# Building one-hot pairs for eight tokens at a time, with new schedule constants

## The chip, the cores and the metric

The kernel runs on one core of one Trainium2 chip. The metric is the device time of one execution in microseconds (us), taken as the median of several runs. TensorE does the matrix products, VectorE and ScalarE the elementwise work, GpSimd issues the gathering transfers, and the queues of SyncE and ScalarE issue the other transfers.

## The reference

A two-layer decoder trunk over 512 tokens plus 16 meta tokens, width 1024, all in float32. Layer 0 mixes with causal pooling, layer 1 with stick-breaking attention over a shared K and V. Behind each stands a PEER feed-forward, which is what the change touches:

```python
def peer(h, w_query, sub_keys, u, v):        # per chunk of tokens
    q = einsum('btd,dq->btq', hx, w_query)   # 8 heads, 2 halves of 128
    s = einsum('bthpc,hpnc->bthpn', q, sub_keys)
    top_s, top_i = top_k(s, 16)              # per half, of 128 sub-keys
    cand = top_s[..., 0, :, None] + top_s[..., 1, None, :]
    best_s, best_pos = top_k(cand, 16)       # of 256 candidates
    expert = i1 * 128 + i2                   # the two sub-key indices of each
    gate = softmax(best_s)
    act = gelu(hx . u[expert])
    return sum(gate * act * v[expert])
```

There are 128 x 128 = 16384 experts a layer, and each token uses 8 heads x 16 = 128 of them.

## The kernel before

**Two ways to the experts.** Of the four tiles of 128 tokens, three are *dense*: every one of the 16384 experts is computed for all 384 tokens and weighted by a gate matrix that is zero nearly everywhere. The fourth tile (`GATHERED`), and in layer 0 the meta tokens, fetch their own experts' rows: one indirect transfer of 128 x 2048 floats (u and v side by side) brings one expert for each of 128 tokens, and VectorE does `prod` (line 355, the dot product), `gwt` (363) and `hx` (367, the weighted sum). These *row steps* are spread over the whole layer.

**Stages of a layer.** (1) The query projection: scores of the sub-keys and their top 16 for each head. (2) The gate stage, lines 600 to 640: for each of the three dense tiles `select` finds the 16 pairs of each head and looks up the two indices i1 and i2, and `build_gates` writes the gate matrix. (3) The value stage: 128 steps `v`, each of 18 matmuls of 512 columns into six accumulators.

**A u step** (`u_parts`, line 314) computes gelu(u . h) for 128 experts and 384 tokens with 24 matmuls: the weights are split into a high and a low part, `w_hi` by ScalarE (line 279) and `w_lo` by VectorE (line 281) once `gating` is set. A layer has 128 u steps. Those that run ahead of the value stage write their result to DRAM (`aout<-ac`) and the value stage loads it again; the rest run within the value stage.

**The gate matrix.** For each token there are 128 chosen pairs (i1, i2) with a gate. With the tokens' pairs on the partitions, the matrix [i2, i1] of one token is the product of the one-hots of i2 with the one-hots of i1 times the gate. The gate is split into two f16 parts, so each token takes two matmuls of 128x128 into a tile `pg`; ScalarE copies four tokens of pg at a time into `stage`, which goes to DRAM as `gout` each 32 tokens.

Before, VectorE builds this for `TG` = 4 tokens in four operations: line 596 the one-hot of i2 into ab[0], line 597 that of i1 into e1, lines 598 and 599 e1 times the two gate parts into ab[1] and ab[2]. `place` issues the matmuls `GLAG` = 2 groups later. ab has three buffers, e1 two.

**The index look-up** (lines 439 to 445) compares the position with 0..15 into a tile `oh` of 2048 elements, multiplies it by the indices and sums; oh has a buffer of its own.

**The order of work** in the gate stage is written out by a plan. `gate_stream` yields a cost in us for each piece of VectorE work. td adds it, times `DVE_SLACK`; tu adds 0.5 for each placed group and ucost/4 for each quarter of a u step; quarters are issued while tu is behind td. Row steps are issued while their own clock tr is behind td, each adding 18/8 to tr and 4.7/8 to td, and four of them make a row; they stop when fewer than `QUIET` groups are left. With `pinned` set, TensorE keeps this order. `issue_after` holds a row's VectorE operations behind the latest marked VectorE operation (`vmark`). Fewer u steps in the gate stage mean as many more in the value stage. In the projection, `ucost` also decides how many u steps fill in.

Of the kernel before, what the change touches and what calls it, by code (L numbers as in the profile page):

```python
# [20 lines left out]
P = 128  # L21
# [5 lines left out]
H = 8  # L27
NK = 128
TK = 16
# [5 lines left out]
GSCALE = 32768.0  # L35
NCAND = 80
TB = 32
FRONT = 3
UPARTS = 4
TG = 4  # L40
GLAG = 2
DVE_SLACK = 1.08
KLAG = 3
ALAG = 3
JG = 4
# [5 lines left out]
WQ_PE = (15.5, 12.5)  # L51
GATHERED = (3,)
LEAD = (2, 2)
QUIET = 16


@with_exitstack
def trunk_kernel(ctx: ExitStack, tc: tile.TileContext, x, meta, norm_mix, norm_ffn, pool_w, pool_scale,
                 kv_norm, w_kv, k_norm, w_q, q_norm, w_o, peer_wq, peer_keys, peer_ut, peer_uv, out):
    nc = tc.nc  # L60
    v, sc, pe, gp, sy = nc.vector, nc.scalar, nc.tensor, nc.gpsimd, nc.sync
# [4 lines left out]
    def const(shape, dt, name):  # L66
        return cp.tile(shape, dt, name=name)
# [1 line left out]
    ident = const([P, P], F32, "ident")  # L69
    make_identity(nc, ident)  # L70
    iota_x = const([P, P, 2], F16, "iota_x")
    iota_b = const([P, TK], BF, "iota_b")
    own = const([P, AH], F32, "own")
    rr = const([P, H, NM], F32, "rr")
    gkv = const([P, KC], F32, "gkv")
# [179 lines left out]
    def peer(layer, with_meta, gain, hn_nat, kp, up, finish):  # L255
# [5 lines left out]
        ND = nd * P  # L261
# [6 lines left out]
        with ExitStack() as cl:  # L268
# [3 lines left out]
            vmark, amark, pmark, todo = [], [], [], []  # L272
# [17 lines left out]
            def pin(x):  # L290
                return tc.keep_in_program_order(x) if pinned[0] else x
# [80 lines left out]
            def row_step():  # L372
                if not stepping:
                    if not todo:
                        return False
                    stepping.append(row_steps())
                if next(stepping[0], 0):
                    return True
                stepping.clear()
                return row_step()  # L380

            with ExitStack() as c1:
                tp = c1.enter_context(tc.tile_pool(name="tp", bufs=1, reuse_waits="tile"))
                ps1 = c1.enter_context(tc.tile_pool(name="ps1", bufs=2, reuse_waits="tile", space=PSUM))
# [14 lines left out]
                def select(tmp, outp, tag, tvi, tii, nh, res):  # L399

                    ns = nh * TK

                    def st(name, dt=F32):
                        return tmp.tile([P, H * TK], dt, name=name)[:, :ns]
# [12 lines left out]
                    a, b, u, w = st("da"), st("db"), st("du"), st("dw")  # L417
# [14 lines left out]
                    v.scalar_tensor_tensor(u, a, 16.0, u, ALU.mult, ALU.min)  # L432
                    vmark.append(v.tensor_sub(b, bp, u))
                    yield 3.5
                    tib = tmp.tile([P, nh, 2, TK], BF, name=f"tib{nh}")
                    v.tensor_copy(tib, tii)
                    for half, sel in ((0, a), (1, b)):
                        oh = tmp.tile([P, ns, TK], BF, name=f"oh{nh}")
                        v.tensor_tensor(oh, iota_b.unsqueeze(1).to_broadcast([P, ns, TK]),
                                        sel.unsqueeze(2).to_broadcast([P, ns, TK]), ALU.is_equal)  # L440
                        o4 = oh.rearrange("p (h s) a -> p h s a", h=nh)
                        v.tensor_tensor(o4, o4, tib[:, :, half, :].unsqueeze(2).to_broadcast([P, nh, TK, TK]),
                                        ALU.mult)
                        ir = outp.tile([P, ns], F32, name=f"{tag}i{half}")
                        v.tensor_reduce(ir, oh, AX.X, ALU.add)
                        res.append(ir)
                        yield 6.0 * nh / H
# [11 lines left out]
                    res.append(gate)  # L459
                    yield 1.0  # L460

                ucost = 0.0098 * ND + 0.15
                tq = tr = td = tu = 0.0
                j0 = 0
                with ExitStack() as cq:
# [28 lines left out]
                    for h in range(H):  # L494
                        qts = []
                        for pp in range(2):
                            hp = 2 * h + pp
                            w, whi, wlo = weight(plan.pop(), plan[-1])
# [51 lines left out]

                gb = c1.enter_context(tc.tile_pool(name="gb", bufs=1, reuse_waits="tile"))

                def build_gates(n, i1, i2, gate):

                    pt = ps1.tile([P, 4, P], F32, name="ps1")
                    for q, t in enumerate((i1, i2, gate)):
                        pe.transpose(pt[:, q, :], t, ident)
                    sl = gb.tile([P, 4, P], F16, name="sl", bufs=2)
                    sc.activation(sl[:, :2], pt[:, :2], AF.Copy)
                    sc.activation(sl[:, 2], pt[:, 2], AF.Copy, scale=GSCALE)  # L560
                    gf = gb.tile([P, P], F32, name="gf")
                    v.tensor_copy(gf, sl[:, 2])
                    v.scalar_tensor_tensor(sl[:, 3], pt[:, 2], GSCALE, gf, ALU.mult, ALU.subtract)
                    stages = {}

                    def place(t0, ab):
                        tb = t0 // TB
                        if tb not in stages:
                            stages[tb] = gb.tile([P, NK, TB], F32, name="stage", bufs=2)
                        stage = stages[tb]  # L570
                        pg = ps1.tile([P, TG, NK], F32, name="pg")
                        with tc.issue_after(pmark[-1].ins):
                            for q in range(TG):
                                a, b = divmod(q, 2)
                                pin(pe.matmul(pg[:, q, :], ab[:, 0, a, :, b], ab[:, 1, a, :, b],
                                                 start=True, stop=False))
                                pin(pe.matmul(pg[:, q, :], ab[:, 0, a, :, b], ab[:, 2, a, :, b],  # L577
                                                 start=False, stop=True))
                        pcost[0] += 0.5
                        o = t0 % TB  # L580
                        with tc.issue_after(amark[-1].ins):
                            sc.activation(stage[:, :, o:o + TG].rearrange("p j t -> p t j"), pg, AF.Copy,  # L582
                                                  scale=1.0 / GSCALE)
                        if o + TG == TB:
                            sc.dma_start(gout[:, n * (P // TB) + tb], stage)

                    waiting = []
                    for t0 in range(0, P, TG):
                        ab = gb.tile([P, 3, TG // 2, NK, 2], F16, name="ab", bufs=GLAG + 1)
                        e1 = gb.tile([P, TG // 2, NK, 2], F16, name="e1", bufs=2)  # L590
                        ix = iota_x.unsqueeze(1).to_broadcast([P, TG // 2, NK, 2])

                        def col(q):
                            pair = sl[:, q, t0:t0 + TG].rearrange("p (a b) -> p a b", b=2)
                            return pair.unsqueeze(2).to_broadcast([P, TG // 2, NK, 2])
                        v.tensor_tensor(ab[:, 0], ix, col(1), ALU.is_equal)  # L596
                        v.tensor_tensor(e1, ix, col(0), ALU.is_equal)  # L597
                        v.tensor_tensor(ab[:, 1], e1, col(2), ALU.mult)  # L598
                        vmark.append(v.tensor_tensor(ab[:, 2], e1, col(3), ALU.mult))  # L599
                        waiting.append((t0, ab))  # L600
                        if len(waiting) > GLAG:
                            place(*waiting.pop(0))
                        yield 1.34
                    for wq in waiting:
                        place(*wq)

# [2 lines left out]
                def gate_stream():  # L609
                    if with_meta:  # L610
                        res = []
                        yield from select(gb, gr, "gm", tvm, tim, 1, res)
                        gather_rows(NT, 0, *res, TK, ym, True)
                    for n, i in enumerate(dense):
                        res = []
                        yield from select(gb, gb, "gd", tv[i], ti[i], H, res)
                        for cost in build_gates(n, *res):
                            blocks[0] -= 1
                            yield cost

                pcost = [0.0]
# [434 lines left out]
```

## Time and profile before

| | |
|---|---|
| median of 3 runs | 3105.51 us (3097.78 to 3110.7) |
| the profiled execution: time, span | 3103.72 us, 3102.0 us |
| busy TensorE, its weight loads | 2942.2 us (95%), 2605.9 us (84%) |
| busy VectorE | 2446.9 us (79%) |
| busy ScalarE, GpSimd | 1349.8 us (44%), 734.9 us (24%) |
| mean granted clock of TensorE | 0.979 |

The span is the time from the first to the last instruction of the profiled execution. Busy shares are averages over stages with different limits; the records of neighbouring operations of one engine overlap a little, so a duration isn't always what an operation costs in a row of them. A "releaser" is what an engine's idle time ended with.

### The profile page before, as it was taken

Reading aid. Unit: us, or ns where it says so; the run is one execution under the profiler, and the core shown is the slowest. Engines: PE = TensorE matmul, PEld = TensorE weight load, DVE = VectorE, ACT = ScalarE, POOL = GpSimd, SP = SyncE. Lnnn points to the kernel's source line nnn. Section 1 sums busy time; section 2 is a strip of 40 time slices with the busy share of each in tenths; the row PEclk is TensorE's granted clock in tenths of the full one; section 3 lists DMA queues with packets and bytes.
Section 4 is the critical chain, followed back from the end, with each engine's and each line's share of the span. In section 5 each row is a group of like instructions: output and inputs, shape, how many; then the busy total and the mean of one; then the engine's idle time right before and its main releaser. Section 6 shows DMA issues by size and latency. Waiting matters only on the chain.

```text
span 3102.0 us, 45813 instructions
## 1 busy us (share of the span) xinstructions
PE 2942.2 (95%) x16514; PEld 2605.9 (84%) x16514; DVE 2446.9 (79%) x5636; ACT 1349.8 (44%) x2184; POOL 734.9 (24%) x704
## 2 busy tenths in 40 slices
PE   8988988999999999999999989798899999999999
PEld 7887888888888888879965778788888888888887
DVE  3999998987777778786456469999988777777765
ACT  3343655633333333344456334355655333333333
POOL 3431521311111111114245244322321111111100
PEclk9999999999999999999999999999999999999999
DMA  3535877899898998862100344477879998989875
GB/s 128 183 123 202 301 272 274 307 377 326 312 335 300 343 317 324 285 219 73 55 1 1 109 171 145 155 266 278 296 270 346 356 324 311 338 301 335 308 251 162
DMA packets 286709, 758.52 MB, mean 245 GB/s; under 512 B 23185, under 2 KB 176785, under 8 KB 248337
## 3 DMA queue, kind: packets, MB, share of 16 engines
q1 hardware_dynamic: 222544, 390.92, 37.5%
q0 software_dynamic: 39168, 285.23, 25.0%
q10 hardware_dynamic: 24768, 79.44, 6.5%
q8 instruction: 129, 2.11, 0.3%
q14 instruction: 100, 0.81, 0.1%
HBM read 673.99 MB, written 81.53 MB: 244 GB/s over the span
## 4 chain that ended last, share of the span: by engine, by line
PE 68%; DVE 26%; DMA 2%; issue 2%; ACT 2%; POOL 0%; SPq 0%; DVEq 0%; ACTq 0%; POOLq 0%
PE y L693 33%; PE psu L314 21%; DVE w_lo L281 3%; PE pp L124 2%; PE pp L125 2%; PE pp L123 2%; DVE prod L355 2%; DVE ab L599 2%; DVE ab L598 2%; DVE e L597 2%; DVE hx L367 2%; DVE ab L596 2%; DVE mr L395 1%; DVE ti L397 1%; DVE ti L394 1%
## 5 line engine op out<-in xcount | busy, mean ns | idle before, releaser
L343 POOL DMA_INDIRECT row<-in_peer_uv_dram,ei x272 | 429.0, 1577 | 1751.3 <-DVE hx L367 1406.2
L314 PE MATMUL psu<-n_hi,w_lo 128*128 128x384 f32 x2048 | 705.9, 345 | 64.4 <-DVE w_lo L281 62.4
L314 PE MATMUL psu<-n_hi,w_hi 128*128 128x384 f32 x2048 | 722.2, 353 | 11.5 <-ACT ac L321 7.2
L314 PE MATMUL psu<-n_lo,w_hi 128*128 128x384 f32 x2048 | 706.0, 345 | 0.6 <-DVE n_lo L118 0.6
L279 ACT ACTIVATE w_hi<-w 128x1024 fp32r<-128x1024 f32 x288 | 305.0, 1060 | 480.2 <-PE psu L314 378.3
L693 PE MATMUL y<-v_hi,wt_hi 128*128 128x512 f32 x1536 | 474.0, 390 | 1.2 <-ACT wt_hi L685 0.8
L693 PE MATMUL y<-v_hi,wt_lo 128*128 128x512 f32 x1536 | 473.9, 390 | 0.2
L693 PE MATMUL y<-v_lo,wt_hi 128*128 128x512 f32 x1536 | 473.5, 389 | 0.5 <-DVE v_lo L679 0.5
L314 PEld LDWEIGHTS psu<-n_hi,w_lo 128*128 128x128 f32 x2048 | 396.5, 194 | 73.5 <-DVE w_lo L281 71.1
L314 PEld LDWEIGHTS psu<-n_hi,w_hi 128*128 128x128 f32 x2048 | 394.9, 193 | 17.5 <-ACT ac L321 7.5
L314 PEld LDWEIGHTS psu<-n_lo,w_hi 128*128 128x128 f32 x2048 | 395.3, 193 | 5.5 <-DVE n_lo L118 1.1
L685 ACT ACTIVATE wt_hi<-wt 128x384 fp32r<-128x384 f32 x256 | 134.3, 525 | 576.4 <-PE y L693 294.9
L686 DVE TENSOR_TENSOR wt_lo<-wt,wt_hi 128x384 fp32r<-128x384 f32 x256 | 142.5, 557 | 263.8 <-ACT wt_hi L685 263.8
L693 PEld LDWEIGHTS y<-v_lo,wt_hi 128*128 128x128 f32 x1536 | 288.2, 188 | 61.8 <-DVE v_lo L679 1.3
L693 PEld LDWEIGHTS y<-v_hi,wt_lo 128*128 128x128 f32 x1536 | 288.1, 188 | 61.3 <-DVE wt_lo L686 1.1
L367 DVE SCALAR_TENSOR_TENSOR hx<-row,gwt,hx 128x1024 f32<-128x1024 f32 x256 | 334.5, 1307 | 2.1
L355 DVE SCALAR_TENSOR_TENSOR prod<-row,hnat 128x1024 bf16<-128x1024 f32 x272 | 335.7, 1234 | 0.4 <-DMA row<-in_peer_uv_dram,ei 0.4
L281 DVE TENSOR_TENSOR w_lo<-w,w_hi 128x1024 fp32r<-128x1024 f32 x228 | 278.1, 1220 | 72.8 <-ACT w_hi L279 71.3
L693 PEld LDWEIGHTS y<-v_hi,wt_hi 128*128 128x128 f32 x1536 | 286.6, 188 | 54.1 <-ACT wt_hi L685 1.4
L679 DVE TENSOR_TENSOR v_lo<-v,v_hi 128x1024 fp32r<-128x1024 f32 x256 | 312.2, 1220 | 6.9 <-ACT v_hi L678 6.8
L678 ACT ACTIVATE v_hi<-v 128x1024 fp32r<-128x1024 f32 x256 | 270.8, 1058 | 16.5 <-DMA v<-in_peer_uv_dram 13.6
L582 ACT ACTIVATE stage<-pg 128x512 f32<-128x512 f32 x192 | 211.7, 1133 | 103.5 <-PE pg L577 102.4
(313 smaller groups left out, 4518.0 us busy)
## 6 DMA issues: line engine op xcount, KB each, us to landing
w<-in_peer_ut_dram SPq DMA_DIRECT2D x256, 512.0 KB
v<-in_peer_uv_dram SPq DMA_DIRECT2D x256, 512.0 KB
gout<-stage ACTq DMA_DIRECT2D x24, 2048.0 KB
gt<-gout SPq DMA_DIRECT2D x64, 768.0 KB
aout<-ac ACTq DMA_DIRECT2D x148, 192.0 KB
ac<-aout SPq DMA_DIRECT2D x148, 192.0 KB
w<-in_peer_wq_dram SPq DMA_DIRECT2D x32, 512.0 KB
wn<-in_w_kv_dram SPq DMA_DIRECT2D x8, 1024.0 KB
```

Source lines behind the costliest of these rows:

```text
L279: amark.append(sc.activation(whi, w, AF.Copy))
L281: vmark.append(v.tensor_sub(wlo, w, whi.bitcast(F32)))
L314: m = pin(pe.matmul(ps[:, :ND], a[:, k, :], b[:, k, c0:c0 + ND], start=st, stop=en))
L343: gp.indirect_dma_start(out=row, out_offset=None, in_=peer_uv, in_offset=bass.IndirectOffsetOnAxis(ap=item[1], axis=0))
L355: v.scalar_tensor_tensor(prod, row[:, :D], 1.0, hn_nat[i], ALU.mult, ALU.mult, accum_out=dot)
L367: v.scalar_tensor_tensor(acc, row[:, D:], wt, acc, ALU.mult, ALU.add)
L582: sc.activation(stage[:, :, o:o + TG].rearrange("p j t -> p t j"), pg, AF.Copy, scale=1.0 / GSCALE)
L678: amark.append(sc.activation(vhi, v32, AF.Copy))
L679: vmark.append(v.tensor_sub(vlo, v32, vhi.bitcast(F32)))
L685: sc.activation(whi, wt, AF.Copy)
L686: vmark.append(v.tensor_sub(wlo, wt, whi.bitcast(F32)))
L693: pe.matmul(y[n][half], wp[:, ts], vq[:, half * 512:(half + 1) * 512], start=st, stop=en)
```

## The change

One-hots are made for eight tokens in three operations: one comparison writes the one-hots of i1 and i2 into a tile `hot`, and two multiplications write i1's one-hots times the two gate parts into `weighed`. For that the transposed columns `sl` are laid out by groups of eight tokens. hot and weighed have GLAG + 1 = 2 buffers each. The index look-up of the dense tiles takes a buffer of hot as its oh, and the look-up's small constants become f16. `place` now issues two pg tiles of four tokens. Constants of the plan change too: TG, GLAG, DVE_SLACK, QUIET, ucost, and the costs of a group and of a placement.

```diff
-TG = 4
-GLAG = 2
-DVE_SLACK = 1.08
+TG = 8
+GLAG = 1
+DVE_SLACK = 1.35
-QUIET = 16
+QUIET = 8
-    iota_b = const([P, TK], BF, "iota_b")
+    iota_b = const([P, TK], F16, "iota_b")
-                    tib = tmp.tile([P, nh, 2, TK], BF, name=f"tib{nh}")
+                    tib = tmp.tile([P, nh, 2, TK], F16, name=f"tib{nh}")
-                        oh = tmp.tile([P, ns, TK], BF, name=f"oh{nh}")
+                        if nh == H:
+                            oh = hot_tile().rearrange("p w a k b -> p (w a k b)").rearrange("p (n a) -> p n a", a=TK)
+                        else:
+                            oh = tmp.tile([P, ns, TK], F16, name=f"oh{nh}")
-                ucost = 0.0098 * ND + 0.15
+                ucost = 0.0111 * ND
+                def hot_tile():
+                    return gb.tile([P, 2, TG // 2, NK, 2], F16, name="hot", bufs=GLAG + 1)
-                    sl = gb.tile([P, 4, P], F16, name="sl", bufs=2)
-                    sc.activation(sl[:, :2], pt[:, :2], AF.Copy)
-                    sc.activation(sl[:, 2], pt[:, 2], AF.Copy, scale=GSCALE)
-                    gf = gb.tile([P, P], F32, name="gf")
+                    sl = gb.tile([P, P // TG, 2, 2, TG], F16, name="sl", bufs=2)
+                    for q in range(2):
+                        sc.activation(sl[:, :, 0, q, :], grouped(pt[:, q, :]), AF.Copy)
+                    sc.activation(sl[:, :, 1, 0, :], grouped(pt[:, 2, :]), AF.Copy, scale=GSCALE)
+                    gf = gb.tile([P, P], F32, name="dw")
...
-                        pg = ps1.tile([P, TG, NK], F32, name="pg")
-                            for q in range(TG):
-                        pcost[0] += 0.5
+                        for t in range(t0, t0 + TG, 4):
+                            pg = ps1.tile([P, 4, NK], F32, name="pg")
+                                for q in range(4):
+                            pcost[0] += 0.47
...
-                        ab = gb.tile([P, 3, TG // 2, NK, 2], F16, name="ab", bufs=GLAG + 1)
-                        e1 = gb.tile([P, TG // 2, NK, 2], F16, name="e1", bufs=2)
-                        ix = iota_x.unsqueeze(1).to_broadcast([P, TG // 2, NK, 2])
-                        v.tensor_tensor(ab[:, 0], ix, col(1), ALU.is_equal)
-                        v.tensor_tensor(e1, ix, col(0), ALU.is_equal)
-                        v.tensor_tensor(ab[:, 1], e1, col(2), ALU.mult)
-                        vmark.append(v.tensor_tensor(ab[:, 2], e1, col(3), ALU.mult))
-                        waiting.append((t0, ab))
+                        hot = hot_tile()
+                        weighed = gb.tile([P, 2, TG // 2, NK, 2], F16, name="weighed", bufs=GLAG + 1)
+                        c = sl[:, t0 // TG].rearrange("p q w (a b) -> p q (w a) b", b=2)
+                        v.tensor_tensor(hot.rearrange("p w a k b -> p (w a) k b"),
+                                        iota_x.unsqueeze(1).to_broadcast([P, TG, NK, 2]),
+                                        c[:, 0].unsqueeze(2).to_broadcast([P, TG, NK, 2]), ALU.is_equal)
+                        for part in range(2):
+                            m = v.tensor_tensor(weighed[:, part], hot[:, 0],
+                                                c[:, 1, part * TG // 2:(part + 1) * TG // 2].unsqueeze(2).to_broadcast(
+                                                    [P, TG // 2, NK, 2]), ALU.mult)
+                        vmark.append(m)
+                        waiting.append((t0, hot, weighed))
-                        yield 1.34
+                        yield 2.44
```

## Rows read from the trace of the kernel before

**Rows 1.** The page, part 4: the chain that ended last, by engine and line.
```profile
PE 68%; DVE 26%; DMA 2%; issue 2%; ACT 2%; POOL 0%; SPq 0%; DVEq 0%; ACTq 0%; POOLq 0%
PE y L693 33%; PE psu L314 21%; DVE w_lo L281 3%; PE pp L124 2%; PE pp L125 2%; PE pp L123 2%; DVE prod L355 2%; DVE ab L599 2%; DVE ab L598 2%; DVE e L597 2%; DVE hx L367 2%; DVE ab L596 2%; DVE mr L395 1%; DVE ti L397 1%; DVE ti L394 1%
```

**Rows 2.** Stretches: length, each engine's busy us (instructions), clock, DMA share, GB/s.
```profile
56.00:255.00 199.00, 177.91 (x1231) 173.40 (x1229) 173.78 (x884) 80.96 (x144) 75.25 (x39) 0.93 0.41 144
255.00:612.00 357.00, 320.33 (x2209) 296.41 (x2210) 344.43 (x887) 202.80 (x263) 100.63 (x31) 0.97 0.78 280
612.00:1381.00 769.00, 764.08 (x3659) 670.09 (x3658) 603.78 (x867) 292.28 (x480) 115.74 (x106) 1.00 0.89 317
...
1783.00:1998.00 215.00, 191.09 (x962) 169.73 (x962) 180.64 (x868) 87.08 (x123) 91.50 (x45) 0.96 0.43 150
1998.00:2347.00 349.00, 313.31 (x2151) 290.34 (x2150) 334.45 (x840) 194.48 (x253) 87.85 (x29) 0.95 0.78 276
2347.00:3102.00 755.00, 747.55 (x3564) 655.09 (x3562) 564.76 (x805) 281.08 (x452) 97.53 (x87) 1.00 0.86 304
```

**Rows 3.** The chain in order of time, value stage: start, us, what.
```profile
742.87 4.23 PE psu L314 x24
747.10 8.18 PE y L693 x36
```

**Rows 4.** VectorE's groups by line, gate stage of layer 0.
```profile
L281 DVE TENSOR_TENSOR w_lo<-w,w_hi 128x1024 fp32r<-128x1024 f32 x61 | 74.2, 1216 | 11.0 <-ACT w_hi L279 10.8
L596 DVE TENSOR_TENSOR ab<-iota_x,sl 128x512 f16<-128x512 f16 x96 | 40.1, 418 | 1.1 <-PE pg L577 1.1
```

**Rows 5.** In order of time, gate stage of layer 0: start, us, engine, line.
```profile
331.92 0.23 PE L575 MATMUL pg<-ab 128*128 128x128 f16 x1
...
332.37 0.42 PE L314 MATMUL psu<-n_hi,w_hi 128*128 128x384 f32 x1
...
337.67 1.22 DVE L281 TENSOR_TENSOR w_lo<-w,w_hi 128x1024 fp32r<-128x1024 f32 x1
338.81 1.22 DVE L355 SCALAR_TENSOR_TENSOR prod<-row,hnat 128x1024 bf16<-128x1024 f32 x1
...
339.95 0.42 DVE L598 TENSOR_TENSOR ab<-e,sl 128x512 f16<-128x512 f16 x1
340.29 0.41 DVE L599 TENSOR_TENSOR ab<-e,sl 128x512 f16<-128x512 f16 x1
...
341.63 0.15 DVE L363 TENSOR_TENSOR gwt<-ga,g_1gate 128x1 f32<-128x1 f32 x1
341.70 0.41 DVE L596 TENSOR_TENSOR ab<-iota_x,sl 128x512 f16<-128x512 f16 x1
342.03 1.27 DVE L367 SCALAR_TENSOR_TENSOR hx<-row,gwt,hx 128x1024 f32<-128x1024 f32 x1
343.23 0.41 DVE L597 TENSOR_TENSOR e<-iota_x,sl 128x512 f16<-128x512 f16 x1
...
411.17 1.22 DVE L442 TENSOR_TENSOR oh<-oh,tib 128x2048 bf16<-128x2048 bf16 x1
412.31 1.22 DVE L281 TENSOR_TENSOR w_lo<-w,w_hi 128x1024 fp32r<-128x1024 f32 x1
```

**Rows 6.** Waits in the gate stages (TensorE twice, VectorE in layer 0): total, times, longest.
```profile
PE psu L314 <- DVE w_lo L281: 26.2, 14, 3.8
...
DVE w_lo L281 <- ACT w_hi L279: 10.8, 7, 3.0
DVE ab L596 <- PE pg L577: 1.1, 2, 0.9
...
PE psu L314 <- DVE w_lo L281: 27.1, 11, 7.7
```

**Rows 7.** VectorE's groups by line, whole span, shapes apart.
```profile
L439 DVE TENSOR_TENSOR oh<-iota_b,db 128x2048 bf16<-128x2048 bf16 x6 | 13.7, 2283 | 0.0
```

**Rows 8.** The page, part 6: transfers issued.
```profile
aout<-ac ACTq DMA_DIRECT2D x148, 192.0 KB
```

More of the change, by code (lines that the diff above doesn't have):

```diff
@@ L557, in build_gates, with grouped, place @@
                         pe.transpose(pt[:, q, :], t, ident)
-                    sl = gb.tile([P, 4, P], F16, name="sl", bufs=2)
-                    sc.activation(sl[:, :2], pt[:, :2], AF.Copy)
-                    sc.activation(sl[:, 2], pt[:, 2], AF.Copy, scale=GSCALE)
-                    gf = gb.tile([P, P], F32, name="gf")
-                    v.tensor_copy(gf, sl[:, 2])
-                    v.scalar_tensor_tensor(sl[:, 3], pt[:, 2], GSCALE, gf, ALU.mult, ALU.subtract)
+                    sl = gb.tile([P, P // TG, 2, 2, TG], F16, name="sl", bufs=2)
+                    def grouped(t):
+                        return t.rearrange("p (g t) -> p g t", t=TG)
+                    for q in range(2):
+                        sc.activation(sl[:, :, 0, q, :], grouped(pt[:, q, :]), AF.Copy)
+                    sc.activation(sl[:, :, 1, 0, :], grouped(pt[:, 2, :]), AF.Copy, scale=GSCALE)
+                    gf = gb.tile([P, P], F32, name="dw")
+                    v.tensor_copy(grouped(gf), sl[:, :, 1, 0, :])
+                    v.scalar_tensor_tensor(sl[:, :, 1, 1, :], grouped(pt[:, 2, :]), GSCALE, grouped(gf), ALU.mult,
+                                           ALU.subtract)
                     stages = {}
-                    def place(t0, ab):
+                    def place(t0, hot, weighed):
                         tb = t0 // TB
@@ L570, in place @@
                         stage = stages[tb]
-                        pg = ps1.tile([P, TG, NK], F32, name="pg")
-                        with tc.issue_after(pmark[-1].ins):
-                            for q in range(TG):
[L574 to L578, printed above, removed]
-                        pcost[0] += 0.5
[L580 to L584, printed above, removed]
+                        for t in range(t0, t0 + TG, 4):
+                            pg = ps1.tile([P, 4, NK], F32, name="pg")
+                            with tc.issue_after(pmark[-1].ins):
+                                for q in range(4):
+                                    a, b = divmod(t - t0 + q, 2)
+                                    for part in range(2):
+                                        pin(pe.matmul(pg[:, q, :], hot[:, 1, a, :, b], weighed[:, part, a, :, b],
+                                                      start=part == 0, stop=part == 1))
+                            pcost[0] += 0.47
+                            o = t % TB
+                            with tc.issue_after(amark[-1].ins):
+                                sc.activation(stage[:, :, o:o + 4].rearrange("p j t -> p t j"), pg, AF.Copy,
+                                              scale=1.0 / GSCALE)
+                        if t0 % TB + TG == TB:
                             sc.dma_start(gout[:, n * (P // TB) + tb], stage)
@@ L588, in build_gates @@
                     for t0 in range(0, P, TG):
-                        ab = gb.tile([P, 3, TG // 2, NK, 2], F16, name="ab", bufs=GLAG + 1)
-                        e1 = gb.tile([P, TG // 2, NK, 2], F16, name="e1", bufs=2)
-                        ix = iota_x.unsqueeze(1).to_broadcast([P, TG // 2, NK, 2])
-                        def col(q):
-                            pair = sl[:, q, t0:t0 + TG].rearrange("p (a b) -> p a b", b=2)
-                            return pair.unsqueeze(2).to_broadcast([P, TG // 2, NK, 2])
-                        v.tensor_tensor(ab[:, 0], ix, col(1), ALU.is_equal)
-                        v.tensor_tensor(e1, ix, col(0), ALU.is_equal)
-                        v.tensor_tensor(ab[:, 1], e1, col(2), ALU.mult)
-                        vmark.append(v.tensor_tensor(ab[:, 2], e1, col(3), ALU.mult))
-                        waiting.append((t0, ab))
+                        hot = hot_tile()
[4 more added lines that the diff above has]
+                                        c[:, 0].unsqueeze(2).to_broadcast([P, TG, NK, 2]), ALU.is_equal)
+                        for part in range(2):
+                            m = v.tensor_tensor(weighed[:, part], hot[:, 0],
[3 more added lines that the diff above has]
+                        waiting.append((t0, hot, weighed))
                         if len(waiting) > GLAG:
                             place(*waiting.pop(0))
-                        yield 1.34
+                        yield 2.44
                     for wq in waiting:
```

## The prediction

> **What bounds the kernel now.** I first read the chain that ended last [rows 1]. It is mostly TensorE, but a quarter is VectorE, and the four one-hot lines 596 to 599 alone hold about 7% of the span, over 200 us. So somewhere TensorE waits for them. The stretches [rows 2] say where: the first is the query projection of layer 0, the second its gate stage, the third its value stage, and three more for layer 1. In the value stages TensorE is busy 764.1 of 769 us and 747.6 of 755. In the gate stages VectorE is the fuller engine, 344.4 of 357 us and 334.5 of 349, while TensorE stands idle 36.7 us and 35.7 us and its granted clock is 0.97 and 0.95. The waits [rows 6] name the idle time: most of it is TensorE's psu matmuls waiting for w_lo, VectorE's low part of an expert weight. VectorE's own idle time in there is 12.6 and 14.6 us, in layer 0 nearly all of it w_lo waiting for ScalarE's w_hi.
>
> So in the gate stages VectorE sets the end, in the value stages TensorE does. An expert step ("u", 24 matmuls) takes 4.23 us of TensorE wherever it stands, and two value steps take 8.18 us [rows 3]. A u done in a gate stage therefore shortens the value stage by 4.23 us, and is free in so far as it falls into TensorE's idle time.
>
> **Price of a VectorE operation.** The mean of one [rows 4] is not its price here. In the order of time [rows 5] L598 starts at 339.95 and L599 at 340.29, so a 128x512 f16 operation listed with 418 ns costs about 0.34 us from start to start: five in a row, from 339.95 to 341.63, take 1.68 us, 0.336 each. The next one starts before the last has ended. The 128x2048 multiplication of 16-bit data, L442, starts at 411.17 and the next operation at 412.31: 1.14 us. A straight line between the two puts 128x1024 at 0.336 + 0.268 = 0.604 us. In the same way w_lo is 1.14 us, and a gathered row costs 1.14 (prod) + 0.07 (gwt) + 1.20 (hx) = 2.41 us.
>
> **The change, part by part.**
>
> *One-hots.* Eight tokens took 8 x 0.336 = 2.69 us; now one comparison of 2048 elements and two multiplications of 1024 take 1.14 + 2 x 0.604 = 2.35 us. The element count is the same; only five starts are saved. Over 48 groups of eight in each layer that is 16.3 us, in both 33 us of VectorE. This assumes that the wider comparison keeps the pace of L596 [rows 4], whose operands are all f16, as the new one's are. The other end: the comparison L439 of 128x2048, whose sel is f32 in the code, takes 2283 ns [rows 7], 1.06 us more than L442; at that pace the sum would turn by 96 x 1.06 = 102 us.
>
> The Trainium skill (VectorE: DVE Perf Modes, section on where the cycles go for 2048 bf16 elements) counts some 150 cycles of set-up in each operation, and its section on terms says that the next operation can't issue until the pipe is empty. By that, 8 x 0.43 us would become 1.22 + 2 x 0.70, and the saving an estimated 80 us in place of 33. Its time for 2048 elements, about 1224 ns, agrees with the length of L442 here, but the starts in [rows 5] stand 0.08 us closer than the lengths, so I take the rows.
>
> *Schedule.* More comes from the constants. A gate stage is a plan: each yield adds its cost times DVE_SLACK to td, and u quarters are issued until tu has caught up, each for ucost/4, each placed group for pcost. Per layer the base cost was 3 x (22.5 + 32 x 1.34) x 1.08 = 211.8 and becomes 3 x (22.5 + 16 x 2.44) x 1.35 = 249.2 (layer 0 has 6 more for the meta tokens, times the slack). Row steps stretch td by 1/(1 - 4.7/18) = 1.353, except over the last 64 tokens (QUIET halves as the groups double, so that is as before). Layer 0 comes to td = 287 before and 339 after, layer 1 to 279 and 328. Less the placements (48, now 45) and divided by ucost (3.913, now 4.262), followed through the loops with their rounding: u in the gate stage 62 to 70 and 60 to 67; gathered rows 29 to 35 and 28 to 34. The larger ucost also takes one u out of each projection (10 to 9, 16 to 15). The count for before can be tested: every u ahead of the value stage spills one ac, 10 + 62 + 16 + 60 = 148, as [rows 8] have it. After it must be 161.
>
> *Value stages.* 13 u fewer: 13 x 4.23 = 55 us less. TensorE is 99% busy there, so this is real time. Rows are paced some 9% faster by the larger ucost, but six fewer are left in each layer; DMA share 0.89 and VectorE at 604 of 769 us leave that cover.
>
> *Gate stages.* VectorE: -33 + 15 u x 1.14 (17) + 12 rows x 2.41 (29) = +13 us on the engine that sets the end. TensorE takes 15 x 4.23 = 63 us more in. Does that fit? In layer 0, 70 u x 4.23 = 296, and 96 placements of four tokens at 0.45 (from the first pg matmul at 331.92 to the next u matmul at 332.37) = 43, make 339 us against VectorE's 344 + 7 = 351; in layer 1, 283 + 43 = 326 against 341. VectorE stays the longer, but by little, where each side can now make the other wait. DMA moved 280 GB/s x 357 us = 100 MB in layer 0's stage; 8 more weights of 0.52 MB, 8 spills of 0.20 and 6 rows of 1.05 are 12 MB, which takes its share from 0.78 to an estimated 0.87, less than the 0.89 that the value stage bears.
>
> *Waits that are added.* Two hot buffers of eight tokens replace three of four, so the comparison of a group waits for TensorE to finish the group two back. Behind it on VectorE stand w_lo and the row operations, and TensorE waits for w_lo. Before, this wait came to 1.1 us in layer 0 [rows 6]. The one-hots of the selection take a hot buffer as well, and so wait for the last groups of the tile before; some 14 us of candidate work lies between, which covers it; uncovered it is at most a u, 4.23 us, for each of six tiles. The price of tighter coupling lies between nothing and, as an upper end, a doubling of VectorE's 27 us of idle time plus the six u (25 us): 52 us. I take 5, since the row of before is near zero and since the two engines' sums still differ by 12 us a layer or more.
>
> *Projections.* One u less in each. In layer 0 TensorE has 21 idle us of 199 there, in layer 1, 24 of 215 [rows 2]; 0 to 8 us, I take 4.
>
> The rest of the edits (f16 in place of bf16 in iota_b and tib, gf under another name, one more ScalarE copy in each of six tiles) I cost at nothing: u matmuls queue ahead of the transposed tile's first group. Uncovered, at an estimated 0.5 us each (a little over the 0.42 us listed for 512 elements), it is 3 us. The 13 more spills and reloads of 192 KB are 5 MB in 758.
>
> **Sum.** 3103.7 (the profiled execution; 1.8 under the median of the runs) - 55 + 13 + 5 - 4 = 3063 us, or -1.3%. A change under 0.5% (15 us) could not be told from none with this kernel's runs.
>
> **Rivals.**
>
> *A deeper gain.* If an operation cost VectorE its listed length, eight tokens would go from 8 x 0.418 = 3.34 us to 1.22 + 2 x (0.418 + 0.268) = 2.59, and VectorE would save 72 us, not 33. The gate stages would then fall to TensorE's 339 and 326, with some 7 us of idle time left in each: 679 in place of 357 + 349 = 706, so -27 where the forecast has +18, and the time is 3018. For it: the listed 418 ns. Against it: every pair in [rows 5]. 0.10. The rule of the Trainium skill's page VectorE: DVE Perf Modes speaks for this rival.
>
> *Given back.* The added u and rows make the gate stages as much longer as the value stages shrink: coupling at its upper end, 52 us in place of 5, gives 3110. For it: the two engines' sums lie within 4% of each other, and TensorE waits of up to 7.7 us for w_lo are there already [rows 6]. Against it: the waits of before come from VectorE being full, and TensorE's extra work falls into 72 us of idle time. With half of it the time is some 3087. I give 0.14 to a result within 0.5%.
>
> *Slower.* The comparison waits for its hot buffer in every group. Place: the first operation of each of 96 groups; price 1 us each, about a quarter of a u, so 96 us, which gives 3063 + 96 = 3159. It decides from 0.43 us a group on (41 us). For it: u quarters of 1.06 us now stand between all placements, and TensorE is no longer the one that waits. Against it: 1.1 us in two waits among 96 groups before [rows 6]. The f32 pace of L439, if the wide comparison had it, has the same price and the same place. Together 0.10.
>
> **Numbers.** Forecast 0.66, with its own range 3040 to 3088; the deeper gain 0.10, given back 0.14, slower 0.10. Time 3063. The range of 8 in 10 reaches from 3025, most of the way to the deeper gain, to 3100, half of the cases given back. Faster by over 0.5%: 0.66 + 0.10 + a little of the middle, 0.77; within 0.5%: 0.13; slower 0.10.
>
> **What would show it.** The comparison at 1.22 us and the products at 0.68 listed, starts 1.14 and 0.60 apart; 161 spills; gate stages some 9 us longer each, value stages 30 and 25 us shorter; TensorE's idle time in the gate stages well under 72 us and its clock there nearer 1. The prediction fails if the comparison shows waits for pg of over 0.4 us a group, if its starts are over 2 us apart, or if the gate stages grow by over 50 us together.

## The result

The changed kernel takes 3091.37 us (median of 11 runs, 3084.74 to 3097.72); in the same sessions the kernel before took 3108.26 us (11 runs, 3097.78 to 3112.46). The ratio is 0.995 [0.9937, 0.9962], some 17 us less. The forecast was 3063 us: the direction holds, the size doesn't, though the time lies in the range. The profiled execution took 3092.34 us, with a span of 3090.6 us, 11.4 under the span before; the difference to 17 is that the profile of before lay under the median of its runs and this one over its own.

These stretches of the changed kernel answer to [rows 2]: the gate stage of layer 0, the first 40 us after it, the whole value stage; then the same of layer 1. Columns as there.

```profile
254.40:627.90 373.50, 340.93 (x2378) 327.47 (x2377) 351.11 (x677) 209.29 (x284) 70.34 (x35) 0.97 0.81 293
627.90:667.90 40.00, 32.23 (x152) 29.32 (x150) 22.04 (x31) 13.78 (x24) 4.82 (x5) 0.87 0.93 329
627.90:1377.90 750.00, 739.55 (x3502) 645.30 (x3500) 581.83 (x840) 282.28 (x462) 125.39 (x101) 0.99 0.89 316
1990.60:2359.60 369.00, 332.13 (x2304) 318.47 (x2305) 342.71 (x633) 201.34 (x274) 70.52 (x36) 0.96 0.80 289
...
2359.60:3090.60 731.00, 721.89 (x3418) 629.14 (x3415) 543.30 (x775) 272.74 (x435) 102.60 (x82) 1.00 0.86 303
```

The kernel before, cut in the same way, by the last pg matmul: gate stage of layer 0, the 40 us after it, gate stage of layer 1.

```profile
254.10:611.10 357.00, 320.00 (x2208) 295.76 (x2207) 344.60 (x889) 202.71 (x262) 101.53 (x31) 0.97 0.78 279
611.10:651.10 40.00, 36.03 (x187) 32.28 (x184) 26.78 (x39) 16.41 (x27) 5.83 (x5) 1.00 0.98 357
...
1996.20:2345.90 349.70, 313.90 (x2150) 290.94 (x2151) 335.15 (x843) 193.38 (x252) 88.73 (x30) 0.95 0.78 277
```

Its value stages so cut take 769.0 and 756.1 us. The gate stages grew by 16.5 and 19.3 us, the value stages shrank by 19.0 and 25.1, the stretch between them (attention and the projection of layer 1) by 3.4. In the gate stages VectorE's busy time rose by 6.5 and 7.6 us; the rest of the growth, 22 us, is VectorE standing idle: 22.4 + 26.3 = 48.7 us, 27.0 before. TensorE took 13 more u and its idle time hardly shrank: 32.6 and 36.9 us, 37.0 and 35.8 before.

VectorE's groups by line, gate stage of layer 0, after; they answer to [rows 4]. Columns: busy us, mean ns of one, idle before and its releaser.

```profile
L281 DVE TENSOR_TENSOR w_lo<-w,w_hi 128x1024 fp32r<-128x1024 f32 x68 | 82.9, 1220 | 17.2 <-ACT w_hi L279 16.7
L608 DVE TENSOR_TENSOR weighed<-hot,sl 128x1024 f16<-128x1024 f16 x96 | 62.3, 686 | 0.5
L604 DVE TENSOR_TENSOR hot<-iota_x,sl 128x2048 f16<-128x2048 f16 x48 | 58.3, 1220 | 2.6 <-PE pg L588 2.6
```

The operations have the predicted lengths, 1.22 and 0.69 us. The comparison, which was to wait for TensorE, waits 2.6 us in 48 groups (5.0 in layer 1). Most of the idle time stands ahead of w_lo.

Waits of the changed kernel (total us, times, longest), as [rows 6]: three of the gate stage of layer 0, then two of layer 1:

```profile
ACT w_hi L279 <- PE psu L314: 74.2, 38, 5.2
...
PE psu L314 <- DVE w_lo L281: 28.0, 14, 7.8
DVE w_lo L281 <- ACT w_hi L279: 16.7, 9, 3.0
...
PE psu L314 <- DVE w_lo L281: 32.3, 13, 4.9
DVE w_lo L281 <- ACT w_hi L279: 18.9, 13, 3.0
```

These waits make a ring: TensorE waits for w_lo, VectorE's w_lo for ScalarE's w_hi, and w_hi for TensorE to leave the buffer of two steps back. In the gate stages together TensorE's wait is 60.3 us (53.3 before in the stretches of [rows 6], 56.3 in stages cut as here), VectorE's 35.6 (23.8). So of the 21.7 us that VectorE stands idle more, 11.8 are w_lo behind w_hi, and 5.7 the comparison behind pg (7.6 in place of 1.9).

The transfers after [rows 8]: 161 spills, as counted.

```profile
aout<-ac ACTq DMA_DIRECT2D x161, 192.0 KB
```

### The profile page after: what moved, and what is told of

Same layout as the page of the kernel before. It is cut to its first block, busy times and chain, and to the rows that moved or that the text cites. A ratio compares the mean times of both kernels' runs of the same rounds, so it can differ in the third digit from the quotient of the medians.

```text
span 3090.6 us, 45463 instructions
## 1 busy us (share of the span) xinstructions
PE 2926.3 (95%) x16514; PEld 2609.5 (84%) x16514; DVE 2412.3 (78%) x5158; ACT 1344.7 (44%) x2190; POOL 694.7 (22%) x702
## 4 chain that ended last, share of the span: by engine, by line
PE 71%; DVE 21%; issue 3%; DMA 2%; ACT 2%; POOL 0%; SPq 0%; DVEq 0%; ACTq 0%; POOLq 0%
PE y L705 32%; PE psu L314 24%; PE pp L124 2%; PE pp L125 2%; PE pp L123 2%; DVE w_lo L281 2%; PE pg L588 2%; DVE weighed L608 2%; DVE hot L604 2%; DVE prod L355 2%; DVE hx L367 1%; DVE mr L395 1%; DVE ti L397 1%; DVE ti L394 1%; DMA w<-in_peer_ut_dram 1%
## 5 line engine op out<-in xcount | busy, mean ns | idle before, releaser
L343 POOL DMA_INDIRECT row<-in_peer_uv_dram,ei x272 | 392.6, 1443 | 1641.8 <-DVE hx L367 1238.5
L314 PE MATMUL psu<-n_hi,w_hi 128*128 128x384 f32 x2048 | 713.2, 348 | 11.8 <-ACT ac L321 7.2
L593 ACT ACTIVATE stage<-pg 128x512 f32<-128x512 f32 x192 | 200.7, 1157 | 79.7 <-PE pg L588 77.3
```

What stands on the lines that cost most here:

```text
L314: m = pin(pe.matmul(ps[:, :ND], a[:, k, :], b[:, k, c0:c0 + ND], start=st, stop=en))
L343: gp.indirect_dma_start(out=row, out_offset=None, in_=peer_uv, in_offset=bass.IndirectOffsetOnAxis(ap=item[1], axis=0))
L593: sc.activation(stage[:, :, o:o + 4].rearrange("p j t -> p t j"), pg, AF.Copy, scale=1.0 / GSCALE)
```

## The experiments

Each median stands beside its ratio to the kernel before on the same chip, whose medians were 3109.4, 3107.0, 3107.2 and 3106.5 us in four sessions. Edits are against the changed kernel where nothing else is said. Stages are given as layer 0 / layer 1.

**Which part does what.** Three runs take the operations and the plan apart.

```diff
 # e1_ops_only: the new operations, the plan of before
-DVE_SLACK = 1.35
+DVE_SLACK = 1.08
-ucost = 0.0111 * ND
+ucost = 0.0098 * ND + 0.15
-pcost[0] += 0.47
+pcost[0] += 0.5
-yield 2.44
+yield 2.68
 # e2_plan_only: the kernel before with DVE_SLACK 1.35, the new ucost, 0.47, yield 1.22
 # e8_slack_150: the changed kernel with DVE_SLACK 1.5
```

> The one-hots of the changed kernel with the plan of the kernel before (its slack, ucost and costs, so 62 and 60 u steps and 29 and 28 rows in the gate stages, 148 spills). Theory A, the two engines wait for each other once both are nearly full: VectorE is the longer by some 40 us a stage here, so most of the 33 us that the one-hots save comes through, 20 to 33 us under the kernel before, that is 3075 to 3088, and so as fast as or faster than the changed kernel at 3091. Theory B, the wider operations with two buffers stall: the saving is lost, 3100 to 3110, with waits for pg before the comparison of over 20 us a stage.

> The one-hots of the kernel before with the schedule constants of the changed kernel (70 and 67 u steps, 35 and 34 rows, 161 spills). By work alone VectorE gets 46 us more in the gate stages and the value stages lose 55: 3095 to 3100. Theory A, coupling costs some 20 us more as soon as both engines are full: 3110 to 3125. Theory B, the plan is what made the changed kernel faster: 3085 to 3095.

> The changed kernel with DVE_SLACK 1.5 in place of 1.35: 79 and 76 u steps and 39 and 37 rows in the gate stages, 179 spills. If VectorE alone set the end of the gate stages, they would grow by 9 u and 4 rows of VectorE time, 20 us each, while the value stages lose 38 each: 3055. Theory A, TensorE is already the one that is full for much of the stage: the gate stages grow by about what the value stages lose, 3085 to 3100.

The operations alone: 3088.8 us, 0.9934 [0.992, 0.9947]. The plan alone: 3098.8 us, 0.996 [0.9946, 0.9974]. More slack: 3096.7 us, 0.9954 [0.9936, 0.9971]. The gate stages of the operations alone and of the plan alone, windows of the two kernels:

```profile
255.00:605.00 350.00, 314.65 (x2205) 300.04 (x2204) 330.69 (x652) 199.64 (x266) 63.49 (x31) 0.97 0.80 283
1993.20:2331.10 337.90, 307.30 (x2152) 293.10 (x2152) 321.09 (x605) 191.00 (x255) 66.19 (x30) 0.95 0.80 286
```

```profile
253.20:634.50 381.30, 347.55 (x2375) 325.24 (x2373) 366.19 (x917) 213.02 (x281) 89.36 (x36) 0.96 0.80 286
1997.20:2368.90 371.70, 338.83 (x2305) 316.57 (x2306) 355.84 (x873) 205.43 (x272) 96.67 (x35) 0.96 0.80 287
```

With the operations alone VectorE is busy 13.9 and 14.0 us less than before (the step said 16.3 in each layer; the stages hold one hx more in layer 0 and one prod more in layer 1), and the gate stages are 7.0 and 11.8 us shorter: the rest became idle time, 27.0 to 36.1 us; 3088.8 lies just above the range of theory A. With the plan alone the stages are 24.3 and 22.0 us longer, VectorE's busy time by 42.3 and its idle time by only 4.0 us, and 3098.8 is what the expectation gives for work alone. The two halves so add 9.1 and 4.0 us of idle time one by one, and 21.7 together. Most of the gain is that of the operations; on top of them the plan brings nothing (3091.4 against 3088.8, not told apart), and neither does more of the same plan (3096.7, in the range of theory A and not told apart from the change): at slack 1.5 VectorE's idle time is 46.8 and 34.3 us. TensorE's idle time hardly answers to any of it: 35.4 / 30.6, 33.8 / 32.9 and 34.3 / 27.9 us in the three runs.

**Does either engine's total set the gate stage?** e9 leaves out the products with the second gate part and uses the first in its place (VectorE does less), e10 leaves out the matmul of the second part (TensorE does less).

```diff
 # e9_one_product
-for part in range(2):
+for part in range(1):        # products; the matmul reads weighed[:, 0] for both parts
 # e10_one_matmul
-for part in range(2):
+for part in range(1):        # pg matmuls, start=True, stop=True
```

> The changed kernel with the second product of each group (the gate's low part) left out; the matmuls of the low part read the high part's product again, so the gates lose that part's value and TensorE's work stays. VectorE loses 48 x 0.60 = 29 us in each gate stage. VectorE alone sets the stage: 3091 - 58 = 3033. Theory A, mutual waits: TensorE's work becomes the longer, some 15 us a stage come through, 3055 to 3070. The stage is TensorE's: 3085 to 3095.

> The changed kernel with the second matmul of each token (the gate's low part) left out; both products are still made. TensorE loses 384 matmuls of 0.057 us, 22 us in each gate stage; VectorE's work stays. VectorE alone sets the stage: 3085 to 3093. Theory A, mutual waits: part of it comes through, 8 to 15 us a stage, 3060 to 3077. The stage is TensorE's: 3091 - 44 = 3047.

3090.0 us, 0.9943 [0.9928, 0.9958], and 3089.5 us, 0.9942 [0.9927, 0.9958]: neither differs from the changed kernel's 3091.4. Windows of the gate stages, e9 and then e10:

```profile
253.00:628.30 375.30, 342.95 (x2374) 330.32 (x2373) 324.89 (x629) 209.35 (x284) 60.29 (x36) 0.95 0.81 291
1987.70:2356.20 368.50, 335.11 (x2305) 321.73 (x2305) 315.57 (x585) 201.08 (x275) 62.53 (x36) 0.96 0.80 289
```

```profile
252.60:629.70 377.10, 326.26 (x1989) 311.62 (x1988) 349.92 (x676) 207.87 (x283) 72.95 (x36) 0.95 0.81 289
1988.50:2353.40 364.90, 319.73 (x1923) 304.74 (x1922) 340.49 (x633) 201.06 (x275) 72.06 (x35) 0.94 0.82 291
```

VectorE lost 26.2 and 27.1 us of work in e9, and its idle time rose to 50.4 and 52.9 us; TensorE lost 14.7 and 12.4 in e10, and its idle time rose to 50.8 and 45.2. The stages stayed within 4.1 us. Neither the theory that VectorE's sum sets the gate stage nor the one that TensorE's does survives, since each run contradicts one of them. Theory A, that mutual waits hold the stage, was expected to let part of the work come through and missed in both runs too: nothing came through. The Trainium skill (Perfetto Trace Analysis, Identifying the Most-Contended Engine) says to work on the engine of highest occupancy first; here that is VectorE at 351 of 373 us, and 26 us less of it gave nothing.

**Two smaller suspects.** e5 takes the row steps out of the early part of the gate stage and raises the slack (a lighter VectorE, fewer transfers). e6 and e7 look at the handover, the first 40 us of the value stage, where TensorE now stands idle 7.8 us at a clock of 0.87 (4.0 us and 1.00 before): e6 was to issue the first two loads of gt from GpSimd instead of SyncE's queue, e7 keeps one more u ahead of the value stage.

```diff
 # e5_rows_later
-DVE_SLACK = 1.35
+DVE_SLACK = 1.5
+                    if blocks[0] > 2 * (P // TG):
+                        tr = td
 # e6_gt_pool
-sy.dma_start(gts[jg], ...)
+(gp if len(gts) < 2 else sy).dma_start(gts[jg], ...)
 # e7_front4
-FRONT = 3
+FRONT = 4                    # and ac stays at five buffers
```

> The changed kernel with row steps held back until the first dense tile's groups are done, and DVE_SLACK 1.5 so that the u steps stay about the same: 70 and 68 in the gate stages, but 24 and 24 rows in place of 35 and 34. VectorE loses 11 and 10 rows of 2.41 us there, about 25 us a stage. If VectorE's work sets the end of the stage, or the two engines' mutual waits, the stages get 15 to 25 us shorter each, and as the value stages are TensorE's the time is 3045 to 3065. If the stage is TensorE's by now, it keeps its length: 3080 to 3095.

> The changed kernel with the first two loads of gt issued from GpSimd's queue in place of SyncE's, where they wait 10 to 12 us for the last gout to land and hold the weight loads behind them. If that hold is what layer 0's value stage lost (19 us shorter in place of 30), TensorE's idle time between the gate and the value stage falls from 7.8 us in layer 0 and 4.7 in layer 1 to some 2 each, and the time by 5 to 12 us, 3079 to 3086. If the loss comes from data that the value steps need anyway, nothing changes: 3088 to 3094.

> The changed kernel with four u steps ahead of the first value step in place of three (FRONT 4, the buffers of ac still five). If TensorE stands idle at the start of layer 0's value stage for want of work while gt waits for gout, one more u step covers 4.2 us of it and the clock stays up: 3080 to 3088. If the loads' order on SyncE's queue is what holds it, nothing is gained: 3088 to 3095.

e5 takes 3108.1 us, 1.0002 [0.9991, 1.0013]: VectorE is busy only 330.8 / 323.4 us in the gate stages, with a DMA share of 0.72 / 0.71, and they still take 381.5 / 377.9 us, while the value stages, with the rows left over for them, are 4.2 and 4.1 us longer than the change's. That is slower than all that was expected: some 20 us less of VectorE's work in each stage again gave nothing, and why the stages grew was not found. e6 moves less than was meant: gts[jg] is set before len(gts) is read, so only the first load of each layer goes to GpSimd (two in the whole trace), and SyncE's queue still waits 14.0 us for gout ahead of the next one, 12.4 in the changed kernel. It takes 3104.4 us, 0.9983 [0.9974, 0.9993], worse than the change: TensorE idles 12.1 and 12.7 us in the two handovers. What both loads off SyncE's queue would give was not tested. e7 takes 3094.4 us, 0.9953 [0.9935, 0.9972], not told apart from the change, though TensorE's idle time in layer 0's handover falls to 5.6 us at a clock of 0.97. The handover's loss goes with the plan: TensorE's idle time there is 4.0 us before and 4.7 with the operations alone, 9.4 with the plan alone, 7.8 with both, 8.2 at slack 1.5. Its cause stays open.

**The ring of waits.** The theory that was left, called C in the expectations that follow: TensorE and VectorE wait for each other u by u, as w_hi and w_lo have two buffers and a weight is split only one step ahead. e11 splits it two steps ahead in the gate stages; the room for a third pair comes from one of the four row buffers. e13 is its control and takes only that row buffer away.

```diff
 # e13_nrow3, and e11_three_weights
-NROW = 4
+NROW = 3
 # e11_three_weights only
-whi = ... bufs=2)            # wlo likewise
+whi = ... bufs=3)
-for kk in (key, following):
+more = ("u", following[1] + 1) if gating[0] and following and following[1] + 1 < NK else None
+for kk in (key, following, more):
 # e12_ops_three_weights: the edits of e11 on e1_ops_only
 # e16_before_three_weights: the edits of e11 on the kernel before
```

> The changed kernel with three buffers of w_hi and w_lo in place of two, the weights of a u step split two steps ahead in the gate stages in place of one, and three row buffers in place of four to make room. Neither 29 us less of VectorE nor 22 us less of TensorE made a gate stage shorter. Theory C: the stage is held by mutual waits, u step by u step, since w_lo of the next step is made at most one step ahead; with two ahead TensorE's 33 to 37 idle us a stage fall to 10 to 20 and the time by 20 to 40 us, 3050 to 3070. Theory D: w_lo is late because VectorE has a queue of selection and row work in front of it, whatever the distance; TensorE's idle time stays over 28 us a stage, 3082 to 3095.

> The changed kernel with three row buffers in place of four and nothing else: the control for the two runs above. A row is needed every 7 to 9 us and takes less than that to land, so nothing changes: 3088 to 3095; if rows come late, VectorE waits for them at prod, 3095 to 3110.

> The same three weight buffers, two steps ahead, and three row buffers on the one-hots with the plan of the kernel before (62 and 60 u steps). Theory C: TensorE's idle time falls here as well, but VectorE's work of 331 and 321 us a stage now sets the end, 10 to 25 us under the version without the buffers, 3065 to 3080. Theory D: 3082 to 3095.

e11 takes 3087.0 us, 0.9937 [0.9917, 0.9958], its control 3127.6 us, 1.0068 [1.0042, 1.0094]: 41 us between them for the third pair and the earlier split that it allows. Windows of the gate stages of e11, then of e13:

```profile
261.60:621.60 360.00, 332.00 (x2350) 320.70 (x2348) 346.62 (x674) 207.12 (x281) 80.78 (x35) 0.98 0.82 299
1996.60:2350.00 353.40, 326.85 (x2308) 314.74 (x2307) 339.72 (x633) 201.02 (x275) 84.49 (x34) 0.98 0.83 298
```

```profile
254.10:630.90 376.80, 342.02 (x2381) 327.90 (x2379) 350.80 (x676) 209.83 (x287) 57.89 (x35) 0.97 0.79 288
2002.20:2378.50 376.30, 339.25 (x2305) 325.46 (x2306) 342.48 (x633) 200.73 (x273) 64.65 (x34) 0.94 0.78 280
```

VectorE's busy time is nearly the same in both, its idle time 13.4 + 13.7 us in place of 26.0 + 33.8, and the stages are 16.8 and 22.9 us shorter (layer 0's projection, at 7.5 us more, takes some of it back; layer 1's value stage is 8.4 us shorter as well, layer 0's 3.4 longer). The wait at the join: layer 0 of e13, then layers 0 and 1 of e11:

```profile
PE psu L314 <- DVE w_lo L281: 28.6, 15, 6.6
...
PE psu L315 <- DVE w_lo L281: 10.3, 2, 9.7
...
PE psu L315 <- DVE w_lo L281: 3.7, 3, 2.0
```

In layer 0 28.6 us became 10.3, in layer 1 28.5 became 3.7. That these waits lengthen the gate stages is so shown against the control. The signs that were named beforehand are mixed: TensorE's idle time fell to 28.0 and 26.6 us and not to 10 to 20, as its waits for weighed rose from 3.9 to 19.3 us, and 3087.0 us lies in the range of theory D and isn't told apart from the changed kernel with its four row buffers, since giving one up costs 36 us, which was expected to cost nothing or at most some 19. That a repeated gap on an engine that should be full can mean too few buffers is what the Trainium skill says (Perfetto Trace Analysis, Optimization Strategy); these runs agree.

e12, the operations with the plan of before and the third pair, takes 3072.9 us, 0.9892 [0.9874, 0.991], the fastest of all here, the two kernels included. It left a question: does the change bring the waits (C1), or did the kernel before already pay for them (C2)?

> The kernel before, one-hots and plan, with three buffers of w_hi and w_lo, weights split two steps ahead and three row buffers. Three row buffers alone cost the changed kernel 36 us; splitting two steps ahead then gave it 41 us and VectorE's idle time in its gate stages fell from 60 to 27 us. Theory C1, the waits step by step hold the changed kernel because its two engines are equally full, while in the kernel before VectorE sets the stage by its own work: little comes back, gate stages 5 to 10 us under 357 and 350 each, 3115 to 3135. Theory C2, the waits held the kernel before as much: 3095 to 3110.

e16 takes 3082.9 us, 0.9924 [0.9894, 0.9953]. Its gate stages, windows:

```profile
261.70:603.40 341.70, 309.72 (x2163) 287.19 (x2161) 341.34 (x888) 200.30 (x258) 104.27 (x30) 0.97 0.79 284
1987.10:2322.30 335.20, 303.31 (x2130) 280.15 (x2129) 332.53 (x842) 194.26 (x251) 104.24 (x29) 0.97 0.79 283
```

VectorE is now busy 341.3 of 341.7 us, and 332.5 of 335.2. C1 falls: the kernel before gains 24 us from the third pair, with a row buffer fewer, more than C2 expected. Of its 27.0 us of VectorE's idle time 23.9 are gone. From e16 to e12 the one-hots are worth 10 us, so there too less than VectorE's 28: in e12 its idle time is 10 us in each stage again. Windows of e12:

```profile
261.30:598.00 336.70, 304.11 (x2160) 292.22 (x2159) 326.58 (x648) 196.67 (x262) 73.34 (x30) 0.95 0.80 287
1982.70:2311.60 328.90, 297.86 (x2131) 285.26 (x2130) 318.92 (x604) 190.64 (x254) 74.33 (x29) 0.97 0.80 289
```

This also bounds what the ring explains. VectorE's wait for w_hi, first layers 0 and 1 of e11, then layer 1 of e16, which has none in layer 0:

```profile
DVE w_lo L281 <- ACT w_hi L279: 10.4, 8, 2.6
DVE w_lo L281 <- ACT w_hi L279: 11.3, 7, 3.0
...
DVE w_lo L281 <- ACT w_hi L279: 2.2, 4, 1.5
```

With the third pair and a row buffer fewer the gate stages of both layers together are 29.8 us shorter than without in the kernel before and 29.1 in the changed one. The two still differ as they did: the stages by 36.5 us (35.8 without), VectorE's idle time by 24.0 (21.7), and the times, 3087.0 and 3082.9, aren't told apart. So the lack of a third pair holds both kernels, but by these runs it is not what sets them apart; only the changed kernel was run with three row buffers alone, so what that buffer is worth to the other isn't known. In e11 w_hi waits for TensorE's psu, 95.5 us, and also for its weight to land, 33.3 us (6.2 in e16); which of the two makes VectorE wait there was not tested.

## Why the prediction went wrong

- **The count of the plan**: right. 161 spills, 68 and 65 w_lo in the two gate stages where 61 and 59 were, 35 and 34 rows.
- **VectorE's work in the gate stages** (+13): right, +6.5 and +7.6 us.
- **Value stages** (30 and 25 us less): right in layer 1 (25.1), short in layer 0 (19.0). There the handover lost 3.8 us more to idle time than before, in its first 40 us, at a clock of 0.87 in place of 1.00, and over the whole stage TensorE stood idle 10.5 us (4.9 before); its busy time fell by 24.5 us and not by the 29.6 of seven u. I had costed that place at nothing. The loss goes with the plan and not with the one-hots; what brings it was not found.
- **Projections** (4): 3.4 in the stretch before layer 1's gate stage, nothing in layer 0's projection.
- **The coupling** ("I take 5, since the row of before is near zero and since the two engines' sums still differ by 12 us a layer or more"): this step failed. Measured: 21.7 us more of idle time of VectorE, below the middle of the bounds 0 and 52, and gate stages 16.5 and 19.3 us longer in place of 9. The row I leaned on, the comparison behind pg, was the wrong one for most of it: that wait grew by 5.7 us. More, 11.8 us, came from the other row of [rows 6], w_lo behind w_hi, a join at which each engine in turn is the late one and which I had read as a sign that VectorE was full. The sums of the engines, 351 and 339 us, were taken as if the smaller one could slip into the gaps of the larger. e9 and e10 show that it can't, as neither sum sets the stage, and e11 and e16 show that the waits of the ring lengthen it in both kernels. TensorE's idle time was no free room: in layer 0 37.0 us before, 32.6 after. Why the change adds these 21.7 us stays open: with a third pair it adds 24.0, and the operations alone add 9.1, the plan alone 4.0. What the runs do show is an order: VectorE's busy time lies on average 23, 18, 15 and 10 us a stage above TensorE's in the kernel before, the plan alone, the operations alone and both, and its idle time in the two stages is 27.0, 31.0, 36.1 and 48.7 us; with the third pair (e16, e12, e11) 30, 22 and 14 us stand beside 3.0, 20.1 and 27.1. That the waits grow as the two sums come close is argued from this and was not tested by itself.
- The sum so goes: 16.7 us of coupling, 1 of VectorE's work, 11 of the value stages and 1 of the stretch between make up the 30 us between the forecast's 41 and the 11.4 of the profiles.

Of the rivals, "given back" named the right term, at less than half of its price; I gave it 0.14, for a result within 0.5%, and the time of 3087 that it names for half is 4 us off. "Slower" fell (7.6 us of waits, no f32 pace). "A deeper gain" fell too: with the operations alone VectorE saved 28 us, not 72, as starts and not lengths count. Of what was to show it, TensorE's idle time "well under 72" failed (69.4), and so did the clock (0.97 and 0.96, 0.97 and 0.95 before). None of the three signs of failure came up, the nearest being the gate stages, which grew by 35.8 us together against 50: none of them watched the join that did wait.

## What to carry to other kernels

Where two in-order engines hand each other work through a pair of buffers, don't add up each one's work and take the larger sum: look at how many waits of both directions the join has already, and give the added waiting a price of its own: here 21.7 us where the two sums came within 11 us of each other, and 4.0 where the same plan left VectorE 17 us or more the fuller. One more pair of buffers and a split one step earlier were worth 41 us against the control here, and 24 us to the kernel before, more than the change itself. Try the halves of a change alone: the operations gave 20.6 us, the plan 10.5, both 17.

## What the hardware showed that was not expected

A VectorE operation that reads the result of the one right before it starts later than an independent one. In order of time, gate stage of layer 0, changed kernel (start, us, engine, line):

```profile
597.82 1.22 DVE L604 TENSOR_TENSOR hot<-iota_x,sl 128x2048 f16<-128x2048 f16 x1
598.95 1.22 DVE L281 TENSOR_TENSOR w_lo<-w,w_hi 128x1024 fp32r<-128x1024 f32 x1
600.09 1.22 DVE L355 SCALAR_TENSOR_TENSOR prod<-row,hnat 128x1024 bf16<-128x1024 f32 x1
...
602.44 1.22 DVE L604 TENSOR_TENSOR hot<-iota_x,sl 128x2048 f16<-128x2048 f16 x1
603.69 1.29 DVE L608 TENSOR_TENSOR weighed<-hot,sl 128x1024 f16<-128x1024 f16 x2
604.92 1.23 DVE L604 TENSOR_TENSOR hot<-iota_x,sl 128x2048 f16<-128x2048 f16 x1
```

The row's product, which needs nothing of w_lo, starts 1.14 us after it, 0.08 before its listed end. The w_lo behind the hot of 597.82 needs nothing of it either and starts 1.13 us after it; weighed, which reads hot, starts 1.25 us after hot, 0.03 behind the end. So eight tokens in a row take 604.92 - 602.44 = 2.48 us and not the predicted 2.35. The rule of the Trainium skill that I set aside (VectorE: DVE Perf Modes, Terms), that the next operation waits until the pipe is empty, fits the dependent pair here and not the independent one, if the listed end is taken for the moment when the pipe is empty; whether it is, no run here shows.

And the row buffers: three in place of four cost the changed kernel 36 us (e13 against it), most of it in layer 1, where the value stage is 747.8 us in place of 731.0. VectorE there waits for the gathered rows, as it does for 67.1 us in layer 0's value stage, which is only 6.4 us longer; how much of the 36 us these waits make is not shown. Waits of e13, layer 1's value stage:

```profile
DVE prod L355 <- DMA row<-in_peer_uv_dram,ei: 70.1, 24, 6.3
```

The third pair of weights was paid for with this buffer, so what it would give with four row buffers was not measured.
